# A hybrid recurrent layer with Strassen products: who adds the weight blocks

## The chip, the cores and the metric

The kernel runs on one core of a Trainium2 chip. All weights and inputs lie in HBM when it starts, and the results go back to HBM. The metric is the device time of that core in microseconds (us), from one launch. Five engines work beside each other: TensorE (PE, with its weight loads listed as PEld), VectorE (DVE), ScalarE (ACT), GpSimd (POOL) and SyncE (SP), which here issues most of the loads. Each engine has a queue of its own and runs it in order.

## The reference

One layer for 1024 prompt tokens, 16 learned meta tokens ahead of them and 64 decode tokens (8 sequences of 8), so 1104 tokens, with 1024 channels:

```python
xn = rms_norm(x, gains[0])
proj = xn @ w_in                                  # 1024 x 8192
u, gate_a, q, f, i, og, m_a, m_b = jnp.split(proj, split_idx, axis=-1)
uc, conv_new = causal_conv(u, conv_buf, conv_w, conv_b)
h, h_last = rg_lru(uc, h0, ...)                   # a linear recurrence over the tokens
y_a = h * jax.nn.gelu(gate_a)
o, S_new = hgrn2(q, f, i, S0, lb, is_prompt)      # 8 heads with a 128 x 128 state, chunks of 32
y_b = rms_norm(o, gnorm) * jax.nn.silu(og)
mixed = sigmoid(m_a) * (y_a @ w_branch_a) + sigmoid(m_b) * (y_b @ w_branch_b)
x = x + rms_norm(mixed @ w_out, gains[1])
hn = rms_norm(x, gains[2])
ff = jnp.square(jax.nn.relu(hn @ w_up)) @ w_down  # 1024 -> 4096 -> 1024
x = x + rms_norm(ff, gains[3])
```

Everything is float32. Outputs are x and the new states of the convolution and of both recurrences.

## The kernel before

*Products.* A float32 operand is split into a high and a low float16 part, and a product is made of three matmuls (high by high, high by low, low by high; `prod`, lines 269 to 277). Most weights are worked off as pairs of slabs: two slabs of 128 output columns by 1024 inputs, seen as a 2 x 2 matrix of blocks A11, A12, A21, A22 (512 inputs by 128 columns each). By Strassen's scheme in Winograd's form a pair takes seven block products where plain multiplication takes eight. For this, four sums of weight blocks are wanted:

S1 = A21 + A22, S2 = S1 - A11, S3 = A11 - A21, S4 = A12 - S2.

The seven weight operands are S1, S3, A11, S2, A22, S4 and A12, and PE works through them in this order. Each block product has 12 matmuls, and each pair goes over the tokens in two halves, so it has 2 x 7 x 12 = 168 matmuls of 276 (in the output projection and the MLP 272) columns. `pair` (from line 279) does so for the input projection and the branches, `pairc` (from line 1401) for the MLP. The products land in PSUM banks (q, pd), and ACT and DVE combine them: ACT copies the first product to v and the third to u, DVE adds the second to v (line 1414 in the MLP, 290 elsewhere) and the fourth to u, and then the results are made from u, v and the last three products. In the up projection lines 1431, 1432 and 1434 write them to a buffer EB; in the down projection lines 1456 to 1461 add them to facc.

*Weight operands.* `prep` makes a pair's operands while PE works on the pair before. Its generator `gen_pair` is advanced by a step after most products. `raw_dma` (line 156) has SP load two blocks at once, 512 KB, into one of two buffers ws: first A21 and A22, then A11 and A12. POOL makes the sums, all with float32 tiles of 128 x 512 in SBUF: S1 (line 204) and later S2 (217) and S4 (220) in the single buffer sa, S3 (209) in the place of A21. Each block or sum is then split by `w_split`: ACT writes the high half sh (line 175), DVE the low half sl (line 176), into one of 11 slots of the pool opp. A slot comes free when PE has used its operand for the second half of the tokens. There are 67 pairs: 11 for the HGRN heads, 8 for the gates, 8 for the RG-LRU heads, 8 in the two branches, 32 in the MLP (16 up, 16 down). Ten plain units and the output projection's weights have no sums.

*The order of the work.* A scheduler sets the order on each engine; from the output projection on, PE's order is the order in which the code is written. In time: until about 100 us norm and first projections; to 650 HGRN heads (a projection beside the recurrence of the head before); 650 to 900 RG-LRU heads, where line 1021 is the causal convolution over 1128 columns on DVE and line 334 a sum in evacuating a pair; 900 to 1190 the last gates and the branch products; to 1400 output projection, residual, norm and the first MLP pairs; then the MLP in four groups, and the last norm. On POOL's queue are the sums, some element-wise work of the recurrences, small powers for the norms (line 816) and some DMAs (line 985: a head's gated values to DRAM; states as outputs).

Of the kernel before, what the change touches and what calls it, by code (L numbers as in the profile page):

```python
# [67 lines left out]
def layer_kernel(ctx, tc, xT, w_pl, w_pr, w_o, w_up, w_dn, gw, par, sconv, slru, shg,  # L68
# [8 lines left out]
    wst = sbuf(ctx, "wst", 2)  # L77
    asp = sbuf(ctx, "asp")
    opp = sbuf(ctx, "opp", 11, "right")
# [35 lines left out]
    units, raws = [], []  # L115

    def add_unit(kind, src):
        units.append(kind)
        raws.extend([src] if kind != "pr" else [src[:, 0:2], src[:, 2:4]])

# [42 lines left out]
    def raw_get():  # L163
        if not rawq:
            raw_dma()
        return rawq.pop(0)

    def single(pool):
        return (pool.tile([P, 4, P], F16, tag="sh", name=nm("sh")), pool.tile([P, 4, P], F16, tag="sl", name=nm("sl")))
# [8 lines left out]

    def prep(slot=None, eng=None):
        kind = units[st["unit"]]  # L180
        st["unit"] += 1
        eng = eng or POOL
        if slot is None:
            slot = iter(lambda: single(opp), 0)
        ops = {}

        def gen_plain():
            t0 = raw_get()
            ops[0] = w_split(t0[:, 0], next(slot))
            yield  # L190
            ops[1] = w_split(t0[:, 1], next(slot))
            raw_dma()

        def gen_wo():
            t0 = raw_get()
            w_split(t0.rearrange("p b (k c) -> p (b k) c", c=P), next(slot))
            raw_dma()
            yield

        def gen_pair():  # L200
            t0 = raw_get()
            a21, a22 = t0[:, 0], t0[:, 1]
            sa = asp.tile([P, 512], F32, tag="sa", name=nm("sa"))
            eng.tensor_tensor(sa, a21, a22, op=OP.add)  # L204
            ops["S1"] = w_split(sa, next(slot))
            yield
            t1 = raw_get()
            a11, a12 = t1[:, 0], t1[:, 1]
            eng.tensor_tensor(a21, a11, a21, op=OP.subtract)  # L209
            ops["S3"] = w_split(a21, next(slot))  # L210
            yield
            ops["A22"] = w_split(a22, next(slot))
            raw_dma()
            yield
            ops["A11"] = w_split(a11, next(slot))
            yield
            eng.tensor_tensor(sa, sa, a11, op=OP.subtract)
            ops["S2"] = w_split(sa, next(slot))
            yield
            eng.tensor_tensor(sa, a12, sa, op=OP.subtract)  # L220
            ops["S4"] = w_split(sa, next(slot))
            yield
            ops["A12"] = w_split(a12, next(slot))
            raw_dma()

        return ops, {"pl": gen_plain, "wo": gen_wo, "pr": gen_pair}[kind]()
# [52 lines left out]
    def pair(ops, B, c0, w, s0, s1, tk):  # L279
# [17 lines left out]
        prod(b2, ops["S2"], B(4), 4, c0, w, True)  # L297
        DVE.tensor_tensor(u, u, b2, op=OP.add)
        tk(3)
# [3 lines left out]
        prod(b4, ops["S4"], B(2), 4, c0, w, False)  # L303
        s0.one(1, c0, w, u, b4)
        tk(5)
# [14 lines left out]
    class Slab:  # L320
# [3 lines left out]
        def one(self, e, c0, w, a, b=None):  # L324
            d = self.d(c0, w)[:, e]
            if b is not None:
                DVE.tensor_tensor(d, a, b, op=OP.add)
                a = d
            self.post(d, a, e, c0, w)

        def both(self, c0, w, x0, x1):
            d = self.d(c0, w)
            DVE.tensor_tensor(d[:, 0], *x0, op=OP.add)
            DVE.tensor_tensor(d[:, 1], *x1, op=OP.add)
            self.post(d, d, None, c0, w)
# [37 lines left out]
    class SlabU:  # L373
# [3 lines left out]
        def one(self, e, c0, w, a, b=None):  # L377
            t0 = e * HT + c0
            n = min(w, NPR - t0)
            if b is None:  # L380
                ACT.activation(self.up[:, 3 + t0:3 + t0 + n], a[:, :n], AF.Copy)
            else:
                DVE.tensor_tensor(self.up[:, 3 + t0:3 + t0 + n], a[:, :n], b[:, :n], op=OP.add)
                if n < w:
                    def s(x):
                        return x[:, n:].rearrange("p (b s) -> p b s", s=LS)
                    DVE.tensor_tensor(self.sv[:, :, 3:3 + LS], s(a), s(b), op=OP.add)  # L387

# [134 lines left out]
    def x_sums(n):  # L523
# [3 lines left out]

        def out(i, t, a, b):
            hi, lo = tsh[:, i, :, c0:c0 + CT], tsl[:, i, :, c0:c0 + CT]
            (POOL if (n, i) in ((0, 2), (0, 3), (1, 2), (1, 3)) else DVE).tensor_tensor(t, a, b, op=OP.subtract)  # L530
            ACT.activation(hi, t, AF.Copy)
            flush()
            late.append((lo, t, hi))
# [5 lines left out]

        out(0, b11, b12, b11)  # L540
        yield
        out(2, b12, b22, b12)
        yield
        out(1, b22, b22, b11)
        yield
        out(3, b21, b21, b22)
        yield
# [19 lines left out]
    cwk = cst.tile([P, 4, 8], F32, name="cwk")  # L567
    tmp8 = cst.tile([P, 12, 8], F32, name="tmp8")
    identk = cst.tile([P, P], F32, name="identk")
    DVE.tensor_scalar(g0, pt[:, P_G0, :], SX * math.sqrt(D), None, op0=OP.mult)  # L570
# [517 lines left out]

    # operands of the branch products from what the heads have left in DRAM
    ybctx = ExitStack()  # L1090

    def y_prep(s, scale, dh, dl, pool):
# [6 lines left out]
        for k in range(4):  # L1099
# [13 lines left out]
            out(t[:, :, :HW], 0, 2)  # L1113
            POOL.tensor_tensor(b11, b12, b11, op=OP.subtract)
            yield
# [3 lines left out]
            out(b11, 3)  # L1119
            POOL.tensor_tensor(b22, b22, b11, op=OP.subtract)  # L1120
            yield
            out(b12, 5)
            POOL.tensor_tensor(b21, b21, b22, op=OP.subtract)
            yield
# [93 lines left out]
    for p in range(4):  # L1218
# [7 lines left out]
        gens = [prep(slot=iter([wo[2 * p + j]]))[1] for j in range(2)]  # L1226
        begin(eng=POOL)

# [34 lines left out]
    def bsums(tt, b12, b11, b21, b22, eng):  # L1263
        eng.tensor_tensor(tt[0], b12, b11, op=OP.subtract)
        eng.tensor_tensor(tt[1], b22, tt[0], op=OP.subtract)
        eng.tensor_tensor(tt[2], b22, b12, op=OP.subtract)
        eng.tensor_tensor(tt[3], b21, tt[1], op=OP.subtract)

# [101 lines left out]
    for n, (c0, w) in enumerate(WIN):  # L1370
        bgN.drain(n - 2)
        for half in range(2):
# [18 lines left out]
            if n == 0 and half == 0:  # L1391
                ops01 = [take(slot=(single(p) for p in t1), eng=DVE)]
# [8 lines left out]
    def pairc(ops, B, c0, w, fin, hook=None):  # L1401
# [24 lines left out]
    def up_fin(i, eng=DVE):  # L1426
        def fin(b1, b3, b4, u, v, c0, w):
            eb[0] ^= 1
            e = ep.tile([P, 4, CQ], F32, tag=f"EB{eb[0]}", name=nm("EB"))[:, :, :w]
            sc = math.sqrt(SA) / KU  # L1430
            DVE.tensor_tensor(e[:, 3], u, v, op=OP.add)
            DVE.tensor_tensor(e[:, 2], u, b3, op=OP.add)
            ACT.activation(e[:, 2:4], e[:, 2:4], AF.Relu, scale=sc)
            DVE.tensor_tensor(e[:, 0], u, b4, op=OP.add)
            ACT.activation(e[:, 1], b1, AF.Relu, scale=sc)
# [10 lines left out]
    def dn_fin(g, o):  # L1446
        def fin(b1, b3, b4, u, v, c0, w):
            f11, f21, f12, f22 = (mlp["facc"][:, q // 2, 2 * o + q % 2, c0:c0 + w] for q in range(4))
            if g == 0:
                DVE.tensor_tensor(f22, u, v, op=OP.add)  # L1450
                DVE.tensor_tensor(f21, u, b3, op=OP.add)
                DVE.tensor_tensor(f12, u, b4, op=OP.add)
                ACT.activation(f11, b1, AF.Copy)
            else:
                DVE.tensor_tensor(f22, f22, u, op=OP.add)
                DVE.tensor_tensor(f21, f21, u, op=OP.add)
                DVE.tensor_tensor(f12, f12, u, op=OP.add)
# [197 lines left out]
```

## Time and profile before

| | |
|---|---|
| runs | 1977.58, 1978.86, 1981.55 us; median 1978.86 |
| profiled execution | span 1981.6 us, as long as the longest run; nothing measurable lies around it |
| PE | 1792.7 us busy, 90% of the span, 17856 matmuls |
| PEld | 1522.4 us, 77% |
| DVE | 1611.5 us, 81%, 2674 instructions |
| ACT | 1006.8 us, 51%, 2098 |
| POOL | 718.9 us, 36%, 622 |
| DMA | 160 MB, mean 81 GB/s |

PE is the busiest engine but not busy at every moment. The shares are means over stages that differ, so the table of stages (first group below) says more than this one. The four sums of a pair are 264 of POOL's 622 instructions (one pair's four run on DVE).

### The profile page before, as it was taken

The page shows a single profiled execution, that of the slowest core. Times are in us where ns is not written, and L with a number is a line of the kernel's source. Part 1 is how long each engine was busy: PE and PEld are TensorE (multiplying, and loading weights), DVE is VectorE, ACT ScalarE, POOL GpSimd, SP SyncE. Part 2 cuts the span into 40 slices and gives each one's busy share as a digit, 9 for nine tenths or more (in the row PEclk, how much of TensorE's full clock was granted, in tenths as well). Part 3 has the DMA queues.
Part 4 walks back from the last instruction along what each step waited for, and adds up shares of the span by engine and source line. Part 5 has one row for each costly group of instructions (what it writes and reads, how often), then busy time and mean ns, then how long its engine had stood idle before and what let it go on. Part 6 is the DMA issues. An engine that isn't in the chain of part 4 may idle for free. (4 is left out here: it accounts for less than half of the span.)

```text
span 1981.6 us, 43131 instructions
## 1 busy us (share of the span) xinstructions
PE 1792.7 (90%) x17856; PEld 1522.4 (77%) x17856; DVE 1611.5 (81%) x2674; ACT 1006.8 (51%) x2098; POOL 718.9 (36%) x622
## 2 busy tenths in 40 slices
PE   5888999999999988897789899898998999999887
PEld 4777888888888766675678689787887887787776
DVE  7998989888875999979897867788468768767877
ACT  4545555555445677755433445465346335425653
POOL 2532222221324344446553535672322322222242
PEclk9999999999999999999889999899999999999998
DMA  4111121111223111133554522311111111111115
GB/s 153 44 54 46 57 78 57 67 56 51 73 89 113 57 49 68 57 129 133 187 186 175 183 88 71 83 37 54 54 54 44 64 44 54 54 45 53 66 43 159
DMA packets 69092, 160.00 MB, mean 81 GB/s; under 512 B 5792, under 2 KB 39968, under 8 KB 65824
## 3 DMA queue, kind: packets, MB, share of 16 engines
q1 hardware_dynamic: 53056, 125.23, 19.0%
q0 software_dynamic: 6592, 27.00, 3.5%
q10 hardware_dynamic: 9248, 5.02, 1.0%
q8 instruction: 139, 2.28, 0.5%
q14 instruction: 57, 0.47, 0.1%
HBM read 121.18 MB, written 36.06 MB: 79 GB/s over the span
## 5 line engine op out<-in xcount | busy, mean ns | idle before, releaser
L275 PEld LDWEIGHTS <-sh 128*128 128x128 f16 x3920 | 387.9, 99 | 195.9 <-issue 126.0
L276 PEld LDWEIGHTS <-sl 128*128 128x128 f16 x3920 | 388.1, 99 | 80.4 <-DVE sl L176 6.9
L273 PEld LDWEIGHTS <-sh 128*128 128x128 f16 x3920 | 388.8, 99 | 75.3 <-DVE up L387 1.8
L273 PE MATMUL pd<-tsh,sh 128*128 128x276 f16 (+1 forms) x960 | 272.2, 284 | 36.7 <-DVE U L290 14.6
L273 PE MATMUL q<-hoh,sh 128*128 128x272 f16 (+2 forms) x952 | 259.8, 277 | 24.3 <-DVE U L1414 23.9
L176 DVE SCALAR_TENSOR_TENSOR sl<-ws,sh 128x512 f16<-128x512 f32 x288 | 232.0, 829 | 49.7 <-ACT sh L175 49.4
L275 PE MATMUL pd<-tsl,sh 128*128 128x276 f16 (+1 forms) x960 | 272.3, 284 | 0.0
L276 PE MATMUL pd<-tsh,sl 128*128 128x276 f16 (+1 forms) x960 | 272.2, 284 | 0.0
L273 PE MATMUL q<-aoh,sh 128*128 128x272 f16 (+2 forms) x1008 | 260.2, 268 | 11.6 <-DVE U L1414 10.8
L276 PE MATMUL q<-aoh,sl 128*128 128x272 f16 (+2 forms) x1008 | 260.2, 268 | 4.8 <-DVE sl L176 4.8
L275 PE MATMUL q<-aol,sh 128*128 128x272 f16 (+2 forms) x1008 | 260.2, 268 | 0.0
L275 PE MATMUL q<-hol,sh 128*128 128x272 f16 (+2 forms) x952 | 259.7, 277 | 0.4 <-DVE hol L1274 0.4
L276 PE MATMUL q<-hoh,sl 128*128 128x272 f16 (+2 forms) x952 | 259.6, 277 | 0.0
L175 ACT ACTIVATE sh<-sa 128x512 f16<-128x512 f32 x201 | 125.6, 625 | 237.9 <-POOL sa L220 79.5
L220 POOL TENSOR_TENSOR sa<-ws,sa 128x512 f32<-128x512 f32 x66 | 97.2, 1472 | 409.6 <-DVE sl L176 409.6
L273 PE MATMUL pd<-xh,sh 128*128 128x276 f16 (+1 forms) x776 | 219.1, 282 | 22.4 <-DVE U L290 7.8
L276 PE MATMUL pd<-xh,sl 128*128 128x276 f16 (+1 forms) x776 | 219.2, 282 | 0.0
L275 PE MATMUL pd<-xl,sh 128*128 128x276 f16 (+1 forms) x776 | 219.2, 282 | 0.0
L176 DVE SCALAR_TENSOR_TENSOR sl<-sa,sh 128x512 f16<-128x512 f32 x201 | 150.6, 749 | 82.6 <-ACT sh L175 80.7
L175 ACT ACTIVATE sh<-ws 128x512 f16<-128x512 f32 x288 | 168.8, 620 | 91.5 <-POOL ws L209 74.7
L204 POOL TENSOR_TENSOR sa<-ws 128x512 f32<-128x512 f32 x66 | 107.4, 1627 | 150.6 <-DVE sl L176 116.2
L209 POOL TENSOR_TENSOR ws<-ws,ws 128x512 f32<-128x512 f32 x66 | 96.0, 1455 | 135.5 <-DMA ws<-in_w_pr 60.6
(327 smaller groups left out, 4493.9 us busy)
## 6 DMA issues: line engine op xcount, KB each, us to landing
ws<-in_w_pr SPq DMA_DIRECT2D x70, 512.0 KB, 3.5
ws<-in_w_up SPq DMA_DIRECT2D x32, 512.0 KB, 3.4
ws<-in_w_dn SPq DMA_DIRECT2D x32, 512.0 KB, 3.4
th<-th POOLq DMA_DIRECT2D x16, 544.0 KB, 3.6
ys<-y SPq DMA_DIRECT2D x8, 1088.0 KB, 6.5
th<-th SPq DMA_DIRECT2D x8, 1088.0 KB, 6.6
ws<-in_w_pl SPq DMA_DIRECT2D x10, 512.0 KB, 3.6
y<-sg POOLq DMA_DIRECT2D x8, 544.0 KB, 3.1
```

The costliest lines, as they stand in the source:

```text
L175: ACT.activation(hi, src, AF.Copy, scale=SW)
L176: DVE.scalar_tensor_tensor(lo, src, SW, hi, op0=OP.mult, op1=OP.subtract)
L204: eng.tensor_tensor(sa, a21, a22, op=OP.add)
L209: eng.tensor_tensor(a21, a11, a21, op=OP.subtract)
L220: eng.tensor_tensor(sa, a12, sa, op=OP.subtract)
L273: PE.matmul(o, h[:, k, :], bh[:, k, c0:c0 + w], start=first and k == 0, stop=False, skip_group_check=not first)
L275: PE.matmul(o, h[:, k, :], bl[:, k, c0:c0 + w], start=False, stop=False, skip_group_check=not first)
L276: PE.matmul(o, l[:, k, :], bh[:, k, c0:c0 + w], start=False, stop=(k == nk - 1), skip_group_check=not first)
```

## The change

Nothing of the mathematics changes, but the four sums are formed by DMAs. A DMA that POOL issues with `accum_op=OP.add` reads a block from HBM and adds it to what lies in the SBUF buffer. Here it only adds, so the sums are now S1 = A21 + A22, S2 = S1 + A11, S3 = A11 + A21 and S4 = S2 + A12, which stands for other signs in the scheme. The sums on the token side and DVE's combinations of the products are changed to match (add becomes subtract, or the two inputs change places). These edits are in every place where a product is combined; the number and the shapes of these instructions stay.

The buffers are used in this way. SP loads A22 and A11 (512 KB, `raws`) into ws, and A21 alone (256 KB, `sum_load`) into sa, of which there are now two. POOL issues an accumulating DMA that adds A22 to sa: S1. This is done one pair ahead. After the split of S1, POOL adds A11 to sa by DMA (S2), and after the split of S2, A12 (S4). After the split of A11, POOL adds A21 to A11's place (S3); after the split of A22, SP loads A12 into A22's place. The operands are now prepared in the order S1, A11, A22, S2, S3, A12, S4; before it was S1, S3, A22, A11, S2, S4, A12. The order of the products on PE stays. The argument `eng` is gone, so the pair that was summed on DVE goes the same way. Two small constant tiles (tmp8, identk) move to a pool that is released earlier, to make room for the second sa.

The core of the diff:

```diff
-    asp = sbuf(ctx, "asp")
+    asp = sbuf(ctx, "asp", 2)
...
-        raws.extend([src] if kind != "pr" else [src[:, 0:2], src[:, 2:4]])
+        raws.append(src if kind != "pr" else src[:, 1:3])
+        if kind == "pr":
+            prs.append(src)
...
+    def sum_load():
+        if nsum[0] < len(prs):
+            src = prs[nsum[0]]
+            nsum[0] += 1
+            q = asp.tile([P, 512], F32, tag="sa", name=nm("sa"))
+            nc.sync.dma_start(q, src[:, 0])
+            nc.gpsimd.dma_start(q, src[:, 1], accum_op=OP.add)
+            sums.append((q, src))
...
         def gen_pair():
+            if not sums:
+                sum_load()
+            q, src = sums.pop(0)
             t0 = raw_get()
-            a21, a22 = t0[:, 0], t0[:, 1]
-            sa = asp.tile([P, 512], F32, tag="sa", name=nm("sa"))
-            eng.tensor_tensor(sa, a21, a22, op=OP.add)
-            ops["S1"] = w_split(sa, next(slot))
-            yield
-            t1 = raw_get()
-            a11, a12 = t1[:, 0], t1[:, 1]
-            eng.tensor_tensor(a21, a11, a21, op=OP.subtract)
-            ops["S3"] = w_split(a21, next(slot))
-            yield
-            ops["A22"] = w_split(a22, next(slot))
+            sum_load()
+            a, b = t0[:, 0], t0[:, 1]
+            ops["S1"] = w_split(q, next(slot))
+            nc.gpsimd.dma_start(q, src[:, 2], accum_op=OP.add)
+            yield
+            ops["A11"] = w_split(b, next(slot))
+            nc.gpsimd.dma_start(b, src[:, 0], accum_op=OP.add)
+            yield
+            ops["A22"] = w_split(a, next(slot))
+            nc.sync.dma_start(a, src[:, 3])
+            yield
+            ops["S2"] = w_split(q, next(slot))
+            nc.gpsimd.dma_start(q, src[:, 3], accum_op=OP.add)
+            yield
+            ops["S3"] = w_split(b, next(slot))
+            yield
+            ops["A12"] = w_split(a, next(slot))
             raw_dma()
             yield
-            ops["A11"] = w_split(a11, next(slot))
-            yield
-            eng.tensor_tensor(sa, sa, a11, op=OP.subtract)
-            ops["S2"] = w_split(sa, next(slot))
-            yield
-            eng.tensor_tensor(sa, a12, sa, op=OP.subtract)
-            ops["S4"] = w_split(sa, next(slot))
-            yield
-            ops["A12"] = w_split(a12, next(slot))
-            raw_dma()
+            ops["S4"] = w_split(q, next(slot))
...
-        DVE.tensor_tensor(u, u, b2[:, :w], op=OP.add)
+        DVE.tensor_tensor(u, b2[:, :w], u, op=OP.subtract)
```

Where the instructions stand is told by the order on each engine. First POOL, one pair of the down projection (in_w_dn) before: its four sums, and the first of the next pair.

```order
L204 TENSOR_TENSOR sa_21114<-ws_20892 128x512
L209 TENSOR_TENSOR ws_20892<-ws_21012,ws_20892 128x512
L217 TENSOR_TENSOR sa_21114<-sa_21114,ws_21012 128x512
L220 TENSOR_TENSOR sa_21114<-ws_21012,sa_21114 128x512
L204 TENSOR_TENSOR sa_21351<-ws_21129 128x512
```

POOL in the same stage of the changed kernel, where each row is the issue of a DMA (L180 the first sum of the pair after, L222, L225 and L231 the three others):

```order
L231 DMA sa_20630<-in_w_dn 128x512
L180 DMA sa_21117<-in_w_dn 128x512
L222 DMA sa_20880<-in_w_dn 128x512
L225 DMA ws_20774<-in_w_dn 128x512
L231 DMA sa_20880<-in_w_dn 128x512
L180 DMA sa_21354<-in_w_up 128x512
```

The four sums of a pair have become four issues, of which the first belongs to a pair later than the others. Next ACT, over one pair of the down projection before. L175 are the splits (in this order S1, S3, A22, A11, S2, S4 and A12), L1412 copies v and L1416 copies u.

```order
L175 ACTIVATE sh_21116<-sa_21114 128x512
L175 ACTIVATE sh_21121<-ws_20892 128x512
L175 ACTIVATE sh_21125<-ws_20892 128x512
L175 ACTIVATE sh_21131<-ws_21012 128x512
L1412 ACTIVATE U_21018<-q_21014 128x272
L1416 ACTIVATE U_21018<-q_21016 128x272
L175 ACTIVATE sh_21236<-sa_21114 128x512
L1412 ACTIVATE U_21139<-q_21135 128x272
L175 ACTIVATE sh_21241<-sa_21114 128x512
L175 ACTIVATE sh_21245<-ws_21012 128x512
L1416 ACTIVATE U_21139<-q_21137 128x272
```

The same of the changed kernel, where L190 are the splits (S1, A11, A22, S2, later S3, A12, S4), L1426 copies v and L1430 u:

```order
L190 ACTIVATE sh_21357<-sa_21117 128x512
L190 ACTIVATE sh_21362<-ws_21011 128x512
L190 ACTIVATE sh_21367<-ws_21011 128x512
L190 ACTIVATE sh_21372<-sa_21117 128x512
L1426 ACTIVATE U_21258<-q_21254 128x272
L1430 ACTIVATE U_21258<-q_21256 128x272
L190 ACTIVATE sh_21477<-ws_21011 128x512
L1426 ACTIVATE U_21381<-q_21379 128x272
L190 ACTIVATE sh_21481<-ws_21011 128x512
L190 ACTIVATE sh_21487<-sa_21117 128x512
L1430 ACTIVATE U_21381<-q_21379 128x272
```

The splits of S1 and S2 now stand in one row of four, with two others between them and ahead of v's copy, and S4 stands behind A12 where it stood ahead of it.

## Rows read from the trace of the kernel before

**Rows 1.** Stages: length; busy PE, PEld, DVE, ACT, POOL; PEclk, DMA share, GB/s
```profile
50.00:200.00 150.00, 132.58 (x1596) 115.14 (x1597) 140.31 (x191) 79.13 (x154) 58.64 (x35) 0.99 0.14 47
200.00:650.00 450.00, 441.47 (x5054) 387.28 (x5052) 373.98 (x616) 229.12 (x536) 119.75 (x108) 1.00 0.21 72
650.00:900.00 250.00, 215.25 (x1681) 166.43 (x1679) 228.76 (x293) 172.41 (x286) 109.24 (x96) 0.97 0.22 77
900.00:1150.00 250.00, 208.49 (x1677) 168.42 (x1676) 217.72 (x288) 103.70 (x194) 131.31 (x99) 0.94 0.49 171
1200.00:1400.00 200.00, 177.14 (x2032) 159.50 (x2030) 158.44 (x333) 109.54 (x280) 107.66 (x140) 0.94 0.22 64
1400.00:1900.00 500.00, 476.42 (x4014) 395.95 (x4013) 361.02 (x646) 233.12 (x448) 135.91 (x97) 0.98 0.16 54
```
**Rows 2.** PE's waits, 1400 to 1900: us in total, times, longest
```profile
PE q L273 <- DVE U L1414: 22.6, 15, 2.9
```
**Rows 3.** Groups of POOL, whole run: count, busy us, mean ns, idle before
```profile
L204 POOL TENSOR_TENSOR sa<-ws 128x512 f32<-128x512 f32 x66 | 107.4, 1627 | 150.6 <-DVE sl L176 116.2 <-DMA ws<-in_w_pr 30.9 <-DMA ws<-in_w_up 1.8
L217 POOL TENSOR_TENSOR sa<-sa,ws 128x512 f32<-128x512 f32 x66 | 98.4, 1491 | 18.2 <-DVE sl L176 11.8 <-DVE st L815 6.3
L220 POOL TENSOR_TENSOR sa<-ws,sa 128x512 f32<-128x512 f32 x66 | 97.2, 1472 | 409.6 <-DVE sl L176 409.6
L209 POOL TENSOR_TENSOR ws<-ws,ws 128x512 f32<-128x512 f32 x66 | 96.0, 1455 | 135.5 <-DMA ws<-in_w_pr 60.6 <-DMA ws<-in_w_dn 42.8 <-DMA ws<-in_w_up 30.6
```
**Rows 4.** Timeline of DVE and POOL near 748: start us, us, line
```profile
747.65 3.88 DVE L1021 SCALAR_TENSOR_TENSOR uc<-up,cwk,uc 128x1128 f32<-128x1128 f32 x1
...
747.81 1.29 POOL L209 TENSOR_TENSOR ws<-ws,ws 128x512 f32<-128x512 f32 x1
749.05 1.27 POOL L217 TENSOR_TENSOR sa<-sa,ws 128x512 f32<-128x512 f32 x1
```
**Rows 5.** Single lines of DVE, whole run: ns min/median/max, first and last start
```profile
L1021 DVE SCALAR_TENSOR_TENSOR uc<-up,cwk,uc x24: 1368/1380/3875, 645.9 to 844.6; 128x1128 f32<-128x1128 f32 x24
...
L176 DVE SCALAR_TENSOR_TENSOR sl<-ws,sh x288: 657/679/4508, 11.4 to 1918.9; 128x512 f16<-128x512 f32 x144
```
**Rows 6.** Groups of DVE by form, 1400 to 1900
```profile
L1431 DVE TENSOR_TENSOR EB<-U 128x272 f32<-128x272 f32 x24 | 23.2, 966 | 0.1
...
L1434 DVE TENSOR_TENSOR EB<-U,q 128x272 f32<-128x272 f32 x24 | 10.2, 425 | 2.9 <-PE q L276 2.9
```
**Rows 7.** DMAs that POOL issues: line 985, and issues (KB each, us to landing)
```profile
L985 POOL DMA_DIRECT2D th<-th x16: 531/571/577, 571.5 to 973.8; - x16
...
DMA to landing us min/median/max: 3.0/3.6/9.2
...
th<-th POOLq DMA_DIRECT2D x16, 544.0 KB, 3.6
...
out_o_sp<-S POOLq DMA_DIRECT2D x8, 64.0 KB, 1.8
```
**Rows 8.** Groups of DVE by form, 650 to 900
```profile
L1021 DVE SCALAR_TENSOR_TENSOR uc<-up,cwk,uc 128x1128 f32<-128x1128 f32 x22 | 36.7, 1667 | 0.3 <-ACT uc L1018 0.2
...
L176 DVE SCALAR_TENSOR_TENSOR sl<-ws,sh 128x512 f16<-128x512 f32 x36 | 29.4, 820 | 3.9 <-ACT sh L175 3.8
```
**Rows 9.** Groups of DVE by form, 900 to 1150
```profile
L176 DVE SCALAR_TENSOR_TENSOR sl<-ws,sh 128x512 f16<-128x512 f32 x40 | 45.7, 1172 | 7.8 <-ACT sh L175 7.6
```
**Rows 10.** Timeline of ACT, 1568 to 1583: start us, us, line, idle before, releaser
```profile
1570.33 0.63 ACT L175 ACTIVATE sh<-sa 128x512 f16<-128x512 f32 x1 [6.72 <-PE q L275]
1570.86 0.38 ACT L1412 ACTIVATE U<-q 128x272 f32<-128x272 f32 x1
...
1574.12 0.38 ACT L1416 ACTIVATE U<-q 128x272 f32<-128x272 f32 x1
...
1579.62 1.67 ACT L175 ACTIVATE sh<-ws 128x512 f16<-128x512 f32 x3 [2.80 <-POOL ws L209]
1581.19 0.38 ACT L1412 ACTIVATE U<-q 128x272 f32<-128x272 f32 x1
```

More of the change, by code (lines that the diff above doesn't have):

```diff
@@ L111, in advance @@
                 return
-    units, raws = [], []
+    units, raws, prs = [], [], []
     def add_unit(kind, src):
         units.append(kind)
-        raws.extend([src] if kind != "pr" else [src[:, 0:2], src[:, 2:4]])
+        raws.append(src if kind != "pr" else src[:, 1:3])
+        if kind == "pr":
+            prs.append(src)
     npl = npr = 0
@@ L166, in raw_get @@
         return rawq.pop(0)
+    sums = []
+    nsum = [0]
+    def sum_load():
[6 more added lines that the diff above has]
+            sums.append((q, src))
     def single(pool):
@@ L177, in w_split, with prep @@
         return hi, lo
-    def prep(slot=None, eng=None):
+    def prep(slot=None):
         kind = units[st["unit"]]
         st["unit"] += 1
-        eng = eng or POOL
         if slot is None:
@@ L297, in pair @@
         prod(b2, ops["S2"], B(4), 4, c0, w, True)
-        DVE.tensor_tensor(u, u, b2, op=OP.add)
+        DVE.tensor_tensor(u, b2, u, op=OP.subtract)
         tk(3)
@@ L303, in pair @@
         prod(b4, ops["S4"], B(2), 4, c0, w, False)
-        s0.one(1, c0, w, u, b4)
+        s0.one(1, c0, w, b4, u)
         tk(5)
@@ L326, in one @@
             if b is not None:
-                DVE.tensor_tensor(d, a, b, op=OP.add)
+                DVE.tensor_tensor(d, a, b, op=OP.subtract)
                 a = d
@@ L332, in both @@
             d = self.d(c0, w)
-            DVE.tensor_tensor(d[:, 0], *x0, op=OP.add)
-            DVE.tensor_tensor(d[:, 1], *x1, op=OP.add)
+            DVE.tensor_tensor(d[:, 0], *x0, op=OP.subtract)
+            DVE.tensor_tensor(d[:, 1], *x1, op=OP.subtract)
             self.post(d, d, None, c0, w)
@@ L382, in one @@
             else:
-                DVE.tensor_tensor(self.up[:, 3 + t0:3 + t0 + n], a[:, :n], b[:, :n], op=OP.add)
+                DVE.tensor_tensor(self.up[:, 3 + t0:3 + t0 + n], a[:, :n], b[:, :n], op=OP.subtract)
                 if n < w:
@@ L386, in s @@
                         return x[:, n:].rearrange("p (b s) -> p b s", s=LS)
-                    DVE.tensor_tensor(self.sv[:, :, 3:3 + LS], s(a), s(b), op=OP.add)
+                    DVE.tensor_tensor(self.sv[:, :, 3:3 + LS], s(a), s(b), op=OP.subtract)
     def slab_gate(t):
@@ L526, in x_sums, with out @@
         late = []
-        def out(i, t, a, b):
+        def out(i, t, a, b, op=OP.subtract):
             hi, lo = tsh[:, i, :, c0:c0 + CT], tsl[:, i, :, c0:c0 + CT]
-            (POOL if (n, i) in ((0, 2), (0, 3), (1, 2), (1, 3)) else DVE).tensor_tensor(t, a, b, op=OP.subtract)
+            (POOL if (n, i) in ((0, 2), (0, 3), (1, 2), (1, 3)) else DVE).tensor_tensor(t, a, b, op=op)
             ACT.activation(hi, t, AF.Copy)
@@ L538, in flush @@
                 DVE.tensor_tensor(lo, t, hi, op=OP.subtract)
-        out(0, b11, b12, b11)
+        out(0, b11, b11, b12)
         yield
@@ L543, in x_sums @@
         yield
-        out(1, b22, b22, b11)
+        out(1, b22, b22, b11, OP.add)
         yield
-        out(3, b21, b21, b22)
+        out(3, b21, b22, b21)
         yield
@@ L567, in layer_kernel @@
     cwk = cst.tile([P, 4, 8], F32, name="cwk")
-    tmp8 = cst.tile([P, 12, 8], F32, name="tmp8")
-    identk = cst.tile([P, P], F32, name="identk")
+    tmp8 = hg.tile([P, 12, 8], F32, tag="tmp8", name="tmp8")
+    identk = hg.tile([P, P], F32, tag="identk", name="identk")
     DVE.tensor_scalar(g0, pt[:, P_G0, :], SX * math.sqrt(D), None, op0=OP.mult)
@@ L1113, in y_prep @@
             out(t[:, :, :HW], 0, 2)
-            POOL.tensor_tensor(b11, b12, b11, op=OP.subtract)
+            POOL.tensor_tensor(b11, b11, b12, op=OP.subtract)
             yield
@@ L1119, in y_prep @@
             out(b11, 3)
-            POOL.tensor_tensor(b22, b22, b11, op=OP.subtract)
+            POOL.tensor_tensor(b22, b22, b11, op=OP.add)
             yield
             out(b12, 5)
-            POOL.tensor_tensor(b21, b21, b22, op=OP.subtract)
+            POOL.tensor_tensor(b21, b22, b21, op=OP.subtract)
             yield
@@ L1226, in layer_kernel @@
         gens = [prep(slot=iter([wo[2 * p + j]]))[1] for j in range(2)]
-        begin(eng=POOL)
+        begin()
         def chainw(gens=gens, last=cur["gen"]):
@@ L1263, in bsums @@
     def bsums(tt, b12, b11, b21, b22, eng):
-        eng.tensor_tensor(tt[0], b12, b11, op=OP.subtract)
-        eng.tensor_tensor(tt[1], b22, tt[0], op=OP.subtract)
+        eng.tensor_tensor(tt[0], b11, b12, op=OP.subtract)
+        eng.tensor_tensor(tt[1], b22, tt[0], op=OP.add)
         eng.tensor_tensor(tt[2], b22, b12, op=OP.subtract)
-        eng.tensor_tensor(tt[3], b21, tt[1], op=OP.subtract)
+        eng.tensor_tensor(tt[3], tt[1], b21, op=OP.subtract)
     def ebuf(i):
@@ L1391, in layer_kernel @@
             if n == 0 and half == 0:
-                ops01 = [take(slot=(single(p) for p in t1), eng=DVE)]
+                ops01 = [take(slot=(single(p) for p in t1))]
                 gens1 = cur["gen"]
@@ L1430, in fin @@
             sc = math.sqrt(SA) / KU
-            DVE.tensor_tensor(e[:, 3], u, v, op=OP.add)
-            DVE.tensor_tensor(e[:, 2], u, b3, op=OP.add)
+            DVE.tensor_tensor(e[:, 3], u, v, op=OP.subtract)
+            DVE.tensor_tensor(e[:, 2], u, b3, op=OP.subtract)
             ACT.activation(e[:, 2:4], e[:, 2:4], AF.Relu, scale=sc)
-            DVE.tensor_tensor(e[:, 0], u, b4, op=OP.add)
+            DVE.tensor_tensor(e[:, 0], b4, u, op=OP.subtract)
             ACT.activation(e[:, 1], b1, AF.Relu, scale=sc)
@@ L1449, in fin @@
             if g == 0:
-                DVE.tensor_tensor(f22, u, v, op=OP.add)
-                DVE.tensor_tensor(f21, u, b3, op=OP.add)
-                DVE.tensor_tensor(f12, u, b4, op=OP.add)
+                DVE.tensor_tensor(f22, u, v, op=OP.subtract)
+                DVE.tensor_tensor(f21, u, b3, op=OP.subtract)
+                DVE.tensor_tensor(f12, b4, u, op=OP.subtract)
                 ACT.activation(f11, b1, AF.Copy)
@@ L1456, in fin @@
                 DVE.tensor_tensor(f21, f21, u, op=OP.add)
-                DVE.tensor_tensor(f12, f12, u, op=OP.add)
-                DVE.tensor_tensor(f22, f22, v, op=OP.add)
-                DVE.tensor_tensor(f21, f21, b3, op=OP.add)
+                DVE.tensor_tensor(f12, f12, u, op=OP.subtract)
+                DVE.tensor_tensor(f22, f22, v, op=OP.subtract)
+                DVE.tensor_tensor(f21, f21, b3, op=OP.subtract)
                 DVE.tensor_tensor(f12, f12, b4, op=OP.add)
@@ L1477, in layer_kernel @@
     t1 += [t1p] * 3
-    ops01.append(take(eng=POOL))
+    ops01.append(take())
     for n, (c0, w) in enumerate(LCH):
```

## The prediction

> **What bounds the kernel now.** I read the table of stages first [rows 1]. In 200 to 650 us PE is busy 441.5 of 450 us: nothing can be won there. PE loses most in 650 to 900 (250 - 215.3 = 34.8 us; the RG-LRU heads), 900 to 1150 (41.5; the last gates and the two branches), 1200 to 1400 (22.9), 1400 to 1900 (23.6; the MLP) and 50 to 200 (17.4). In the first of these DVE is busy 228.8 of 250 us and ACT 172.4: DVE sets the pace. In 900 to 1150 DVE has 217.7 and POOL 131.3. In the MLP DVE has only 361 of 500 us, yet the waits say that 22.6 us of PE's 23.6 were spent until DVE's line 1414 had run (v + b3, before the fifth product) [rows 2]: DVE comes late there, 15 times in the stage's 25 or so pairs.
>
> What makes DVE late is seen in three more views. POOL runs 66 rows of each of the four sums, 107.4 + 98.4 + 97.2 + 96.0 = 399 us, 6.05 us a pair [rows 3]. In the timeline a DVE row of line 1021 takes 3.88 us while two sums of 1.29 and 1.27 us run; the shortest row of that line is 1.368 [rows 4, 5]. 3.88 - 1.37 = 2.51, nearly the two sums added: DVE stands still while POOL's sum runs. And in the MLP line 1431, which has both inputs in SBUF, takes 966 ns, while line 1434, equal in shape with one input in PSUM, takes 425 [rows 6]. So what the sums cost is DVE time, more than POOL time.
>
> **What the change does, step by step.**
>
> *The sums leave POOL.* 268 rows (one pair's four ran on DVE) go, and POOL is given 268 issues instead. Plain issues of line 985 take 531 to 577 ns [rows 7], so POOL is busy some 268 x 0.57 = 153 us instead of 399. That alone is worth nothing, since POOL has idle time in every stage [rows 1].
>
> *DVE is no longer held up.* 650 to 900: line 1021 is 22 x (1.667 - 1.368) = 6.6 us over its floor, line 176 from ws 36 x (0.820 - 0.657) = 5.9 [rows 5, 8], together 12.5 us in two groups. 36 splits from ws, four to a pair, are nine pairs, so the sums are 9 x 6.05 = 54 of POOL's 109 us: half. At least 6.2 us come back; at most the 34.8 that PE loses. I take the middle, 20, since groups not counted here are lengthened too. 900 to 1150: line 176 from ws alone is 40 x (1.172 - 0.657) = 20.6 us over its floor [rows 5, 9]; ten pairs of sums are 60 of POOL's 131 us, so 9.5 of it; DVE has 32 us of idle time there, so the gain can be nothing, and at most 41.5. I take 12. MLP: line 1431 alone is 24 x (0.966 - 0.425) = 13 us over, and POOL has nothing but sums to do; PE can win 0 to 22.6; I take 10. The two other stages with loss have about ten pairs; by the rate of the three above, (20 + 12 + 10) / (43 pairs x 6.05) = 0.16, they give 10 x 6.05 x 0.16 = 10, of which I take 7, since the first is bound by loads and norms. Sum: 49 us, between 10 and 100.
>
> *What is added and waits.* The landing of an accumulating DMA is not in the trace. POOL's plain DMAs land after 1.8 us (64 KB) and 3.6 (544 KB) [rows 7]. One of 256 KB that also reads what it adds to moves some 512 KB, so I take 3.3, just under the row nearest to it. Bounds: 1.8, and 9.2, the longest landing of line 985 [rows 7]. [...]
>
> Where does ACT stand still for it? In the MLP the scheduler now puts S1, A11, A22 and S2 in a row, ahead of v. Count from the trace: the first product of a pair's second half ends at 1570.3, when PE releases a split, and v is copied at 1570.86 [rows 10]. Matmuls of this stage take 476.4 / 4014 = 0.119 us [rows 1], so a product of 12 takes at most 1.42. The other six end at 1578.8, the next pair's first at 1580.2 (its v is copied at 1581.19), and its fifth, which waits for line 1414, can begin at 1584.5. After the change: u at 1574.12 and S1 behind it, when the fourth product has freed a slot, at 1574.5; its low half on DVE stands behind u and three facc rows, so it ends at about 1576.7 (line 176: 0.7 us); issue and landing 3.3: 1580.0. S2 0.5, v 0.4, the low half of S2 and the add 1.1: 1582.0, 2.5 us before the fifth product. I keep half a microsecond of it for what these counts miss, so a landing up to some 5.3 us costs nothing in the MLP; what is above it is paid by each of 32 pairs. The raw loads, which ACT and POOL wait for now (S3, A22 and A11 begin 2.8 us late at 1579.62 [rows 10]), are one pair further ahead.
>
> Elsewhere the cover is thinner. In the eight branch pairs S2 stands two or three ACT rows behind S1: I charge 7 us. In the last three pairs S4 stands right behind S2 in ACT's queue, and v of the pair that runs stands behind both; their operands are made pair by pair: 3 us. In the HGRN heads S4 is in places four rows behind S2: twelve pairs, 4 us (bounds of the three: 0 and one landing per pair, 23 x 3.3 = 76). Behind a waiting ACT row are PE's evacuations, and behind a waiting POOL issue are the powers of the norms (line 816) and stores; these already stand behind the sums' waits today.
>
> *What costs nothing.* SP has 67 rows more, two 256 KB loads for one of 512 KB; its waits are for DVE, well ahead. At the start POOL's first two issues wait for two 256 KB loads that stand behind all x loads; POOL idles then. Bytes: about 70 MB more from HBM and 70 MB of reading back, while DMA is busy 14 to 49% of a stage [rows 1]; only 900 to 1150 could feel it. Changed signs change no count and no shape on DVE, and tmp8 and identk only move.
>
> *Sum.* 49 - 14 = 35: 1981.6 - 35 = 1946.6 against the profiled execution, which lies 2.7 us above the median: 1944.
>
> **Rivals.**
>
> 1. *The accumulating landing is late (slower).* From about 5.3 us on, each microsecond costs 32 us in the MLP alone, and the gain is gone at 6.4. For it: the operation is in no row; it reads, adds and writes, and all its 128 rows go through 16 engines shared with everything else. Against it: plain landings from POOL have medians of 3.6 or less for twice the bytes. At 7.5: 1944 + 70 = 2014; at 9.2: 2069 and more.
> 2. *The freed DVE time is off the path.* PE is near its own floor in the MLP, and ACT's waits for landings replace its waits for POOL. Half of the relief (24) less a somewhat larger charge (20) leaves 4: 1975. For it: in 900 to 1150 DVE, ACT and POOL form chains, none is full. Against it: in 650 to 900 DVE is full.
> 3. *POOL isn't freed.* Writing descriptors of an add may take POOL as long as the sum did (1.5 us). The sums would still no longer read SBUF, so DVE is relieved; the landing is 0.9 us later, below the 5.3: about 1950.
>
> [...] I give that 4 in 100, inside rival 1's and my own range.
>
> **Chances.** My forecast 0.56, with a range of its own of 1920 to 1968 (60 us gained, or 10); rival 1 0.20; rival 2 0.19; rival 3 0.05. This kernel's measurement tells about 0.2% (4 us) from no change. Of rival 2, 0.07 falls below that, 0.08 within it and 0.04 above. So faster 0.56 + 0.05 + 0.07 = 0.68, same 0.08, slower 0.24. The range of 8 in 10 leaves out most of rival 1 and a little at the lower end: 1916 to 1994.
>
> **What would show it.** Right: the groups that are now lines 1021, 176 and 1431 at their floors (1.37, 0.66, 0.43 us) with few long rows; DVE busy below 205 us in what is now 650 to 900, and that stage about 20 us shorter; accumulating DMAs landing after 2.5 to 4.5 us; PE's wait for the line that is now 1414 halved. Wrong: landings above 5 us, ACT idle before splits of sa in every MLP pair with PE behind it, or DVE rows that stay long with no sum on POOL, which would put the lock down to something else.

## The result and the profile after

The changed kernel takes 1946.2 us (median of four runs, 1939.99 to 1949.67) against 1979.2 before: a ratio of 0.9826, with a 95% interval of 0.9804 to 0.9847. Forecast were 1944 and a range of 1916 to 1994. The profiled execution has a span of 1942.2 us. The total came out 2 us off, and that was luck: the experiments show that neither of the two terms it was made of was right. Both were far larger, and their errors cancelled.

The first part of the page, of the changed kernel: busy time, share of the span and count of each engine.

```profile
PE 1782.7 (92%) x17856; PEld 1520.1 (78%) x17856; DVE 1466.5 (76%) x2670; ACT 1012.5 (52%) x2098; POOL 538.3 (28%) x626
```

DVE does the same work (four rows fewer) in 1466.5 us where it took 1611.5: 145 us less. That is the first sign that more was freed than the 49 us I counted. POOL went from 718.9 to 538.3.

The stages, at the same times as in [rows 1] (the changed kernel gets ahead by up to 56 us, so the same window holds later work); the columns are the same.

```profile
50.00:200.00 150.00, 143.33 (x1758) 127.92 (x1758) 142.46 (x217) 85.49 (x166) 42.83 (x37) 0.97 0.37 86
200.00:650.00 450.00, 444.90 (x5038) 389.81 (x5036) 352.34 (x614) 239.94 (x554) 82.29 (x111) 1.00 0.39 101
650.00:900.00 250.00, 220.67 (x1723) 172.01 (x1722) 224.95 (x307) 173.40 (x293) 100.30 (x109) 0.96 0.51 130
900.00:1150.00 250.00, 221.53 (x2049) 185.72 (x2047) 186.37 (x291) 103.03 (x216) 93.69 (x95) 0.97 0.72 204
1200.00:1400.00 200.00, 187.10 (x1940) 162.98 (x1938) 140.78 (x301) 106.07 (x246) 77.39 (x111) 0.98 0.44 100
1400.00:1900.00 500.00, 462.83 (x3985) 385.79 (x3984) 315.41 (x662) 239.09 (x452) 89.83 (x98) 0.98 0.46 100
```

PE is busier in every stage but the last. In the MLP it fell from 476.4 to 462.8 of 500 us. The waits of PE in that stage say where (us in total, times, longest):

```profile
PE q L287 <- DVE U L1428: 32.8, 20, 3.6
PE q L287 <- ACT sh L190: 2.6, 2, 1.6
```

Line 1428 is what was line 1414. This wait, which I expected to halve, rose from 22.6 us [rows 2] to 32.8. And yet DVE's rows in that stage are at their floor. The evacuation of the up projection, in the same view as [rows 6]:

```profile
L1445 DVE TENSOR_TENSOR EB<-U 128x272 f32<-128x272 f32 x24 | 10.6, 440 | 0.1
L1446 DVE TENSOR_TENSOR EB<-U,q 128x272 f32<-128x272 f32 x24 | 10.4, 435 | 4.5 <-PE q L290 4.5
```

The row with both inputs in SBUF took 966 ns and now takes 440, like its neighbour. The convolution shows the same over the whole run (ns min/median/max), against 1368/1380/3875 in [rows 5]:

```profile
L1035 DVE SCALAR_TENSOR_TENSOR uc<-up,cwk,uc x24: 1384/1390/1444, 627.0 to 811.5; 128x1128 f32<-128x1128 f32 x24
```

So DVE is relieved, and something else holds PE in the MLP. The DMAs that POOL issues in it (KB each, median us from issue to landing):

```profile
sa<-in_w_up POOLq DMA_DIRECT2D x48, 256.0 KB, 4.3
sa<-in_w_dn POOLq DMA_DIRECT2D x48, 256.0 KB, 4.6
...
ws<-in_w_up POOLq DMA_DIRECT2D x16, 256.0 KB, 6.7
...
ws<-in_w_dn POOLq DMA_DIRECT2D x16, 256.0 KB, 6.6
```

The adds to sa (S1, S2, S4) land after 4.3 to 4.6 us where I took 3.3, those to ws (S3) after 6.6 to 6.7. These are medians; one down pair shows what they hide. The timeline of POOL near 1500 us (start, us, line, idle before and what ended it), then ACT's:

```profile
1500.25 0.86 POOL L180 DMA_DIRECT2D sa<-in_w_dn  x1 [13.54 <-DVE facc L1473]
1500.79 1.22 POOL L222 DMA_DIRECT2D sa<-in_w_dn  x1
1501.33 1.57 POOL L225 DMA_DIRECT2D ws<-in_w_dn  x1
1510.04 0.86 POOL L231 DMA_DIRECT2D sa<-in_w_dn  x1 [7.14 <-DVE sl L191]
```

```profile
1499.65 0.63 ACT L190 ACTIVATE sh<-ws 128x512 f16<-128x512 f32 x1 [0.76 <-PE q L289]
1508.39 0.63 ACT L190 ACTIVATE sh<-sa 128x512 f16<-128x512 f32 x1 [8.11 <-DMA sa<-in_w_dn]
1508.93 0.38 ACT L1426 ACTIVATE U<-q 128x272 f32<-128x272 f32 x1
```

Three adds are issued in one bunch, and the one that this pair waits for (L222, S2) stands second, behind the next pair's first (L180). By the code L180 can go once SP's load of A21 into the same buffer has landed (its row names a row of DVE, which ended at about the same time). SP issues that load late, when DVE's last split from that buffer, S4 of the pair before, is over (1496.83), and it lands after 3.2 us in the median:

```profile
1496.86 0.33 SPq L179 DMA_DIRECT2D sa<-in_w_dn  x1
```

S2 lands 7.5 us after its issue, ACT idles 8.1 us for it, and v's copy (L1426) stands behind ACT's split. PE's own rows show what follows:

```profile
1510.14 0.28 PE L287 MATMUL q<-aoh,sh 128*128 128x272 f16 x1 [3.46 <-DVE U L1428]
1510.26 0.28 PE L289 MATMUL q<-aol,sh 128*128 128x272 f16 x1
...
1510.88 0.43 PE L290 MATMUL q<-aoh,sl 128*128 128x272 f16 x1
1511.11 0.43 PE L287 MATMUL q<-aoh,sh 128*128 128x272 f16 x1
```

PE waits 3.46 us, and soon after its matmuls start 0.23 us apart instead of 0.12. A table of two short windows gives the clock (length, busy PE, PEld, DVE, ACT, POOL, then PEclk):

```profile
1513.80:1518.30 4.50, 4.50 (x41) 3.77 (x39) 1.06 (x3) 0.85 (x2) 0.00 (x0) 0.98 0.00 0
1510.10:1513.80 3.70, 3.66 (x18) 2.50 (x18) 2.28 (x6) 0.00 (x0) 0.80 (x1) 0.56 0.42 71
```

Behind the stall the granted clock is 0.56 of full for 3.7 us, and then 0.98 for the next 4.5. In this window PE counts as busy, so (1 - 0.56) x 3.7 = 1.6 us are lost beside the 3.46 that show as idle, by estimate.

### The profile page after: what moved, and what is told of

The parts are those of the page before. It is cut to its first block, busy times and chain, and to the rows that moved or that the text cites. A ratio compares the mean times of both kernels' runs of the same rounds, so it can differ in the third digit from the quotient of the medians.

```text
span 1942.2 us, 43735 instructions
## 1 busy us (share of the span) xinstructions
PE 1782.7 (92%) x17856; PEld 1520.1 (78%) x17856; DVE 1466.5 (76%) x2670; ACT 1012.5 (52%) x2098; POOL 538.3 (28%) x626
## 3 DMA queue, kind: packets, MB, share of 16 engines
q0 software_dynamic: 45184, 97.28, 25.5%
## 5 line engine op out<-in xcount | busy, mean ns | idle before, releaser
L190 ACT ACTIVATE sh<-ws 128x512 f16<-128x512 f32 x288 | 178.6, 626 | 171.3 <-PE q L289 90.1
L191 DVE SCALAR_TENSOR_TENSOR sl<-ws,sh 128x512 f16<-128x512 f32 x288 | 208.7, 727 | 41.5 <-ACT sh L190 38.8
L190 ACT ACTIVATE sh<-sa 128x512 f16<-128x512 f32 x201 | 125.2, 627 | 202.7 <-DMA sa<-in_w_pr 60.0
L852 PE MATMUL pd<-sh,xh 128*128 128x128 f16 (+1 forms) x576 | 103.5, 222 | 2.3 <-ACT F L366 2.0
L854 PE MATMUL pd<-sh,xl 128*128 128x128 f16 (+1 forms) x576 | 103.7, 222 | 0.0
L853 PE MATMUL pd<-sl,xh 128*128 128x128 f16 (+1 forms) x576 | 103.5, 222 | 0.0
```

The lines of the kernel that those rows point to most:

```text
L190: ACT.activation(hi, src, AF.Copy, scale=SW)
L191: DVE.scalar_tensor_tensor(lo, src, SW, hi, op0=OP.mult, op1=OP.subtract)
L852: PE.matmul(po, a, wh[:, k % 4, :], start=(k == 0), stop=False)
L853: PE.matmul(po, a, wl[:, k % 4, :], start=False, stop=False)
L854: PE.matmul(po, b, wh[:, k % 4, :], start=False, stop=(k == KT - 1))
```

## The experiments

All times are medians; ratios are to runs of the kernel before on the same chip. Where two kernels ran on different chips, the ratios are the safer comparison (0.0010 is 2 us).

**The queue.** The theory after reading the trace: S2's add is late because the next pair's first add is ahead of it. The edit moves `sum_load` and ties its issue behind S2's:

```diff
-            sum_load()
             a, b = t0[:, 0], t0[:, 1]
...
-            nc.gpsimd.dma_start(q, src[:, 2], accum_op=OP.add)
+            s2 = nc.gpsimd.dma_start(q, src[:, 2], accum_op=OP.add)
+            sum_load(s2)          # its accumulating DMA inside tc.issue_after(s2.ins)
```

> The changed kernel, with the first add of the next pair (S1) queued on GpSimd behind this pair's S2 add. Theory: in the 12 down pairs of the last three groups the next pair's first add stands ahead of S2's add in GpSimd's queue and on its DMA queue; S2's add then lands after some 7.5 us instead of 3.5 to 4, and each of these pairs takes 24 us instead of about 19.7. With the order turned, down pairs take 19.5 to 20.5 us and the kernel 1946 - 12 x 4 = 1898 us (1890 to 1915). Rival: an accumulating DMA into a buffer that was just split is slow whatever stands ahead of it, and ScalarE's order is the cause; then the down pairs stay at 24 us and the time within 1940 to 1952.

Measured: 1896.3 us, ratio 0.9579 (0.9562 to 0.9596). The same kind of pair in its timeline, POOL only:

```profile
1491.01 0.87 POOL L222 DMA_DIRECT2D sa<-in_w_dn  x1 [12.85 <-DVE sl L192]
1491.82 0.96 POOL L181 DMA_DIRECT2D sa<-in_w_dn  x1
1492.40 1.28 POOL L226 DMA_DIRECT2D ws<-in_w_dn  x1
1496.30 0.87 POOL L232 DMA_DIRECT2D sa<-in_w_dn  x1 [2.62 <-DVE sl L192]
```

The split of S2 starts at 1494.65, 3.6 us after the issue. PE in its two stretches of down pairs is busy 57.90 of 59 and 59.00 of 59 us, with a clock of 1.00; the changed kernel's two stretches stand below them, with 65 of 75 us and a clock of 0.93 to 0.94:

```profile
1477.00:1536.00 59.00, 57.90 (x501) 48.77 (x499) 38.17 (x83) 19.82 (x39) 11.48 (x13) 1.00 0.52 110
...
1653.00:1712.00 59.00, 59.00 (x512) 49.83 (x511) 34.90 (x76) 17.48 (x35) 10.61 (x12) 1.00 0.51 110
```

```profile
1485.00:1560.00 75.00, 65.14 (x523) 52.92 (x521) 40.61 (x89) 20.17 (x39) 11.41 (x13) 0.94 0.45 94
1685.00:1760.00 75.00, 64.83 (x519) 52.73 (x519) 36.06 (x80) 16.92 (x34) 11.41 (x13) 0.93 0.41 88
```

The rival falls. The size was right and its place only in part: by the copies of v (table below) 36 of the 46 us between the two profiled executions come from eight down pairs, 4.5 us each; most of the rest comes earlier.

**The add itself.** Same instructions in the same order, but each DMA overwrites instead of adding, so the sums are left out:

```diff
-            nc.gpsimd.dma_start(q, src[:, 2], accum_op=OP.add)
+            nc.gpsimd.dma_start(q, src[:, 2])
... (all four alike)
```

> The changed kernel with the accumulate flag taken from GpSimd's four DMAs of a pair, so that each overwrites its target: the sums are left out, but the bytes from HBM, the issues, their order and all waits stay. Theory (the bunching of three DMAs on one queue makes the landing late, and the add itself costs little): landings shorten by less than 1 us, and the time is 1935 to 1950. Rival (reading back and adding is what makes the landing late): single landings fall from 4.2 us to about 3.2, bunched ones from 7.5 to 5 or less, the down pairs lose their 4 us, and the time is 1890 to 1915.

Measured: 1874.4 us, ratio 0.9472 (0.9458 to 0.9486). Here my theory fell. The rival held in that landings fall without the add, from 4.6 us in the median to 3.0 (sa) and from 6.6 to 4.1 (ws) in the down projection, but its range did not: the time is 16 us below the 1890 it began at. The landings, to be compared with those of the changed kernel above:

```profile
sa<-in_w_dn POOLq DMA_DIRECT2D x48, 256.0 KB, 3.0
...
ws<-in_w_dn POOLq DMA_DIRECT2D x16, 256.0 KB, 4.1
```

In the medians adding costs 1.6 us of landing here (1.3 in the up projection, 1.0 before the MLP), and 2.5 for S3's DMAs to ws, which stand last in a bunch. The queue's line of the page (packets, MB, share of the 16 engines), of the changed kernel and then of this one:

```profile
q0 software_dynamic: 45184, 97.28, 25.5%
```

```profile
q0 software_dynamic: 28032, 97.28, 14.3%
```

For the same bytes the queue needs 1.6 times the packets and 1.8 times the share of the engines' time. It also holds the other DMAs that POOL issues (27 MB before the change).

**Both.** The new order and no adding:

> The kernel with the next pair's first add queued behind S2's add, with the accumulate flag taken from all of GpSimd's DMAs (the sums are left out, the bytes and waits stay). Theory: a stall in a down pair needs both, a DMA ahead in the queue and a landing lengthened by reading back; where landings are 3 us the order is worth little: 1866 to 1874, against 1874 with the order unchanged. Rival: the order is worth its 50 us by itself, and the flag another 70: below 1850.

Measured: 1871.3 us, ratio 0.9439 (0.9424 to 0.9453); by the ratios 6.5 us from the run before. So most of the two causes is one: the order matters little where the landings are short (3.0 and 4.1 us in the run before). Of the some 76 us between the changed kernel and this one, the order alone gives back 50, and the adding costs some 28 more where the order is right (0.9579 - 0.9439).

**The relief, from the other side.** The kernel before with its sums left out (S1 to S4 split from plain blocks):

```diff
-            eng.tensor_tensor(sa, a21, a22, op=OP.add)
-            ops["S1"] = w_split(sa, next(slot))
+            ops["S1"] = w_split(a21, next(slot))
... (S3, S2 and S4 alike)
```

> The kernel before with the four sums left out (the operands S1 to S4 are split from plain blocks instead): loads, order of operands and products as before. It gives what can be had at most by taking the sums from GpSimd with no DMA in their place. The prediction's term was 49 us, between 10 and 100: 1930 us. Theory: 1925 to 1940, with VectorE's rows at their floors. Rival (the order of the operands and the earlier prefetch are what gained in the change): less than 20 us, 1960 to 1980.

Measured: 1863.2 us, ratio 0.9416 (0.9402 to 0.9430): 116 us, over twice my term and above its upper bound of 100. The theory's range and the rival's both missed it. The page's engines, and two of DVE's groups (line 1016 is the convolution here):

```profile
PE 1757.5 (94%) x17856; PEld 1511.5 (81%) x17856; DVE 1456.1 (78%) x2670; ACT 1014.4 (55%) x2098; POOL 319.1 (17%) x358
```

```profile
L176 DVE SCALAR_TENSOR_TENSOR sl<-ws,sh 128x512 f16<-128x512 f32 x489 | 363.9, 754 | 78.3 <-ACT sh L175 74.9 <-PE q L270 1.2
L1016 DVE SCALAR_TENSOR_TENSOR uc<-up,cwk,uc 128x1128 f32<-128x1128 f32 x24 | 33.3, 1386 | 2.0 <-ACT uc L1013 1.9
```

**Lock or wait.** To tell whether the sums cost VectorE time or make others wait, they are put back with nobody using them:

```diff
             sa = asp.tile([P, 512], F32, tag="sa", name=nm("sa"))
             eng.tensor_tensor(sa, a21, a22, op=OP.add)
-            ops["S1"] = w_split(sa, next(slot))
+            ops["S1"] = w_split(a21, next(slot))
... (S3's sum goes to sa; S2 and S4 are split from a11 and a12)
```

> The kernel before, where GpSimd still makes all four sums from the loaded blocks, in the same shapes, but nobody uses them: S1 to S4 are split from plain blocks, as in the run without sums (1863 us). Only the loads' buffers wait for the sums. Theory (a sum on GpSimd costs because VectorE stands still beside it): VectorE's rows are long again (the up projection's first evacuation row near 0.9 us, the convolution's mean near 1.6), and 60 to 110 of the 115 us are lost again: 1925 to 1975. Rival (the sums cost because ScalarE, VectorE and then TensorE wait for their results): the time stays at 1863 to 1885, with long rows or without.

Measured: 1967.2 us, ratio 0.9926 (0.9909 to 0.9942). Of the 116 us 101 are lost again (0.9926 - 0.9416 of 1980) though nobody waits for a sum. The same lines:

```profile
PE 1782.0 (91%) x17856; PEld 1520.0 (78%) x17856; DVE 1629.7 (83%) x2674; ACT 1012.5 (52%) x2098; POOL 720.2 (37%) x622
```

```profile
L176 DVE SCALAR_TENSOR_TENSOR sl<-ws,sh 128x512 f16<-128x512 f32 x489 | 432.1, 894 | 65.5 <-ACT sh L175 61.4 <-PE q L275 1.3 <-PE q L276 0.7
L1021 DVE SCALAR_TENSOR_TENSOR uc<-up,cwk,uc 128x1128 f32<-128x1128 f32 x24 | 38.7, 1614 | 0.0
```

DVE is busy 1629.7 us, where it was 1456.1 without the sums: 173.6 us more for POOL's 106.1 + 101.8 + 98.9 + 97.8 = 404.6 us of sums (its four groups); 3.3 us of them are DVE's own sums of one pair, so some 170 are left. Splits take 894 ns on average (754 without), the convolution 1614 (1386). The up projection's first row, for which I had expected 0.9 us, stayed at 0.44 in the MLP: the sums, which now run as soon as a load lands, meet other rows there (line 1264 takes 686 ns on average, where it took 460). The theory holds by the time; which row pays is set by when the sums run. The sums still hold the load buffers and stand ahead of other rows in POOL's queue, so not all 101 us need be DVE's. But PE's waits say that most are: those for DVE add up to 148.3 us in the whole run (75.3 without sums, 144.5 before), while ACT's waits for raw loads before splits grow only from 41.1 to 66.8.

**The same, added to the changed kernel.** Ten additions of 128 x 192 on POOL per pair, into a tile that nobody reads:

```diff
+    def dummies(n, ins):
+        with tc.issue_after(ins.ins):
+            for _ in range(n):
+                POOL.tensor_tensor(scr, scr, scr, op=OP.add)
... (five behind S3's add, five behind S4's)
```

> The changed kernel, plus ten additions of 128 x 192 float32 in SBUF on GpSimd per pair, about as long together as the four sums were (6 us); nothing waits for them. Theory (the sums cost VectorE time, since VectorE stands still beside a GpSimd instruction that works on SBUF): the rows of VectorE with SBUF inputs lengthen as before (the first rows of the up projection's evacuation from 0.43 to about 0.9 us), and 25 to 45 us of the gain are lost: 1971 to 1991. Rival (the gain is that ScalarE and VectorE no longer wait for sums in GpSimd's queue, or the other order of the operands): at most 8 us lost, 1940 to 1954.

Measured: 2013.4 us, ratio 1.0150 (1.0109 to 1.0191): 67 us lost, slower than before the change. The dose was too large, as its own row says:

```profile
L86 POOL TENSOR_TENSOR scr<-scr 128x192 f32<-128x192 f32 x670 | 551.1, 823 | 35.8
```

551 us of GpSimd work, not 399; by proportion 399 would cost 49. DVE's busy time rose from 1466.5 to 1569.2, but here too the rows put POOL's DMA issues back, so this run is a weaker witness than the one above. The up projection's first row takes 555 ns in the MLP, not the 0.9 us expected.

**The order of the operands.** The kernel before, with only S1, A11, A22, S2, S3, A12, S4 as the order of preparation:

> The kernel before with only the order of the operands changed to that of the change (S1, A11, A22, S2, S3, A12, S4), sums on GpSimd. Theory: the order by itself gains nothing, 1970 to 1995. Rival (the order is a part of what the change gains): 1940 to 1965.

Measured: 1977.1 us, ratio 0.9973 (0.9963 to 0.9983): some 5 us. The rival falls; the order is a small part. DVE is busy 1647.8 us in this run, 36 more than before, and yet the time is a little shorter: DVE's total alone does not give the time.

Where the time went, by the start of ACT's n-th copy of v (there are 140) in each profiled execution, us:

```
copy of v       1st   31st    49th    73rd    97th   121st   140th
before         95.5  645.3   889.4  1302.8  1542.2  1788.3  1964.2
after          96.5  626.8   852.4  1261.4  1485.7  1755.8  1924.3
new order      96.7  619.3   844.3  1251.1  1477.2  1711.5  1877.9
no sums        91.1  615.1   826.9  1229.9  1450.2  1683.2  1843.4
```

After against before: 56.5 us ahead at the 97th copy, 40 at the end. Between the 97th and 121st the changed kernel loses 24 us against before: 31 in the eight down pairs with S2's add second in the queue, less 7 that it wins in the four up pairs between them. The kernel without sums wins 13 there.

## Why the prediction was right, and where it wasn't

*What bounds the kernel* was read rightly. DVE was late because POOL's sums slow it, as the kernel with unused sums shows (DVE busy 1629.7 us with them, 1456.1 without). The 20 us for 650 to 900 came about as well: from the 31st to the 49th copy of v the changed kernel takes 225.6 us, where it was 244.1, and DVE is busy 200.5 of them.

*"DVE is no longer held up": 49 us* was mis-sized. It measures 116 us with nothing in place of the sums, some 101 of it with no wait on a sum. Two things were wrong in it. I added up the excess of one or two groups in each stage (12.5 us in 650 to 900) and put little on top, whereas the loss is spread over many of DVE's groups (with the unused sums line 1111 takes 1337 ns on average for ybl and line 1274 1201 from EB, without sums the same rows 1107 and 1018); its total busy time, 145 us less after the change, is a better sign, though no price (see the run on the order). And I capped the gain in each stage by PE's idle time in it (22.6 us in the MLP), which made the upper bound of 100. But the stages with stalls had PEclk of 0.94 to 0.98 [rows 1]: a stall can be followed by matmuls at a lower clock, as at 1510 above (0.56 for 3.7 us), and the table counts these as busy. Without sums PE is busy 398.3 of 400 us at a clock of 1.00:

```profile
1400.00:1800.00 400.00, 398.33 (x3439) 336.20 (x3437) 281.32 (x588) 216.41 (x403) 5.32 (x4) 1.00 0.17 58
```

By the copies of v the kernel without sums wins 39 us from the 85th to the 133rd, most of the MLP. In 200 to 650, where "nothing can be won", it wins about 13 us, more than the 8.5 that PE idled there; where the rest comes from is open.

*"POOL is busy some 153 us instead of 399"* was off: an issue takes 0.86 to 1.2 us in the median with adding (0.54 in the run with overwriting), so POOL was freed of 181 us (718.9 to 538.3), not of 246. That is rival 3 in part. The issues don't slow DVE as the sums did: it is busy 1466.5 us with them and 1456.1 with neither sums nor issues. What their length costs by itself no run shows.

*"A landing up to some 5.3 us costs nothing in the MLP"* was right as far as it went. From 1400 to 1485 S2's add is first in its bunch and lands after 3.6 to 3.7 us, and PE waits 0.8 us in all. From 1485 to 1560, in down pairs, it is second (line 222, min/median/max, the early window first):

```profile
DMA to landing us min/median/max: 3.6/3.7/3.7
```

```profile
DMA to landing us min/median/max: 5.9/6.7/7.5
```

What failed is that I let S2's add start as soon as S1 was split, with nothing ahead of it. The order of POOL shown ahead of the prediction has L180 between L231 and L222, in the down pairs, and L180 waits for the load of SP's shown above. I counted what is queued behind a waiting ACT row and a waiting POOL issue, but not what S2's own add is queued behind. In the pair shown, S2's add is issued 4.8 us after u's copy (1496.02), where I counted 2.6, and lands after 7.5 us, 2.2 over the 5.3: together 4.4 us, about what each of the eight pairs loses. That is rival 1 in eight pairs.

*The charges of 7, 3 and 4 us elsewhere* were too small: at the 73rd copy of v, early in the MLP, the changed kernel is already 31.5 us behind the kernel without sums. Adds and their waits together cost 83 us (1946.2 - 1863.2): 50 by the queue, 33 otherwise, of which some 28 go with the adding as such. *Rival 2* (freed DVE time off the path) is refuted by the 1863 us, of which unused sums take 101 away again. L180's issues, with DVE busy for 76% of the span, have a median of 865 ns and a longest of 1220. Why a landing is longer with adding no run shows; the queue's share, 25.5 against 14.3%, goes the same way.

*What would show it.* Lines 1035 and 1445 are at their floors. Line 191 isn't: in 650 to 900 it takes 844 ns from ws, more than the 820 in [rows 8]. POOL's own element-wise rows remain there, and the rows that meet them still grow: of this window's 65 splits, 18 overlap such a row of POOL and take 1352 ns on average, and the other 47 take 687, also those 11 of them that overlap a DMA issue. (Without any sums the splits take 920 ns there.)

So 1946.6 was 1981.6 - 49 + 14; measured it is close to 1979 - 116 + 83.

## What to carry to other kernels

Where GpSimd and VectorE both work on SBUF, look for what GpSimd's instructions cost in all of VectorE's rows and not in the few longest (404.6 us of sums made VectorE's some 170 us longer here), and count the stretch at the lower clock behind one of TensorE's stalls with the stall (3.7 us at 0.56 behind 3.46 here). When a DMA takes a place in a chain, look up what is ahead of it in its own engine's queue as well as what is behind it: a prefetch for the next tile put ahead of this tile's transfer cost 50 us here, and an edit of a few lines that turns the two makes a kernel of 1896 us, 2.6% below the change and 4.2% below the kernel before.

## What was unexpected in the hardware

An accumulating DMA of 256 KB into sa lands 1.0 to 1.6 us later in the median than one that overwrites, and its issue keeps GpSimd 0.86 us instead of 0.54, medians as well. Of the three adds issued in a bunch in the pair shown, the first landed after 3.6 us, the second after 7.5 and the third after 8.2; with the order turned S2's add is the first and lands after 3.6. Sums of 404.6 us on GpSimd lengthened VectorE's work by some 170 us, 0.42 us for each microsecond of sums; beside a DMA issue a split of VectorE took 687 ns as without one.
